# The low part of the MLP's weights: by a negation and an adding transfer, or by a subtraction

## Chip, cores and metric

The kernel runs on one core of one Trainium2 chip. The metric is the time of one execution on the device in microseconds; the lower, the better. Three executions of the kernel before were timed, and their median is the time before.

## What is computed

A trunk of two layers over 512 latent tokens and 256 context tokens, 1024 channels, float32. Each layer has one input projection, three mixers side by side (attention, mLSTM, RG-LRU), one output projection, and an MLP of 4096 channels. The last layer computes latent tokens alone.

```python
for l in range(DEPTH):
    ul, uc = modulate(rms_norm(xl), ...), modulate(rms_norm(xc), ...)
    yl, yc = token_mixing(ul, uc, ..., w_in[l], w_out[l], ...)
    xl = xl + g1l * yl
    xl = xl + g2l * squared_relu_mlp(modulate(rms_norm(xl), sh2l, sc2l), w_ff1[l], w_ff2[l])
    if l < DEPTH - 1:
        xc = xc + g1c * yc
        xc = xc + g2c * squared_relu_mlp(modulate(rms_norm(xc), sh2c, sc2c), w_ff1[l], w_ff2[l])
return rms_norm(xl, final_g)

def squared_relu_mlp(u, w1, w2):
    return jnp.square(jax.nn.relu(u @ w1)) @ w2
```

## The kernel before

Channels lie on the partitions and tokens along the columns. Every large product runs in three passes over parts of its operands: a high part, rounded to the format in which TensorE takes one pass, and a low part, the rest. `PASSES` names them: high by high, high weights by low input, low weights by high input. `dense` goes through the blocks of 128 input channels and gives all three passes of one block before the next one, so the low part of a weight tile is wanted from the third product of the tile on.

A weight tile is 128 partitions by 1024 columns of float32, 512 KB. `split_raw` (L152 to L160) brings one in: a load on SP's queue into `raw`, a cast on ScalarE into the high part `whi` (L158), and a subtraction on VectorE, `raw` less `whi`, into the low part `wlo` (L159). Each of the three names has three buffers. The buffers of `raw` are shared with other weights, among them the modulation weights `modw`, which in layer 0 are loaded beside the MLP and multiplied on VectorE.

Where these tiles are used:

- `ybc`, inside the attention stage: four tiles of `w_outc[l, 1]`, the rows of the output projection that belong to the mLSTM and the RG-LRU. Its products stand between those of the attention (scores `S`, transposes `pT`).
- `out_proj`: tiles of `w_outc[l, 0]`, the rows of the attention heads, in two sweeps over the tokens.
- `mlp`: 32 tiles of `w_ff1c` and 36 of `w_ff2c` in each layer. The first three tiles of `w_ff1c` go into `First` (L430 to L441), whose products follow the modulated input chunk by chunk as `Modulated` makes it; between them stand the sums `nps<-ones,n2acc` of the norm (L221), the reciprocal root `rsq` on POOL (L193), and its spreading over the partitions `nps<-ident,rsq` (L229). The last 8 of the 36 tiles go over the tokens in two sweeps, so that the next norm can begin on the first half while the second is still computed: 256 columns then 512 in layer 0, twice 256 in layer 1.

All products of `dense` are recorded under L186, those of `First` under L440. The order of the instructions on each engine is set by a scheduler that the program is written for; an engine takes its own instructions in that order, and waits where one is not ready. POOL has little to do: the roots of the norms, a few fills, and transfers within the mixers (L807, L917, L919).

Of the kernel before, what the change touches and what calls it, by code (L numbers as in the profile page):

```python
# [19 lines left out]
NK = 8  # L20
# [7 lines left out]
# how fast parts of the program go beside others, by layer  # L28
# [32 lines left out]
def trunk_kernel(ctx, tc, ins, out, dbg=None):  # L61
# [42 lines left out]
    # x^T, chunks of 128 channels, tokens [context | latent]  # L104
# [9 lines left out]
    # adds up rows r, 32 + r, 64 + r, 96 + r  # L114
# [6 lines left out]
    # ------------------------------------------------------------------ interleaving  # L121
    # A part of the program is a generator that yields about how long (us) what it emitted takes.
# [16 lines left out]
    def weave(*gens):  # L139
        """emit parts side by side, at equal pace; a filler only as long as the others last."""  # L140
        at = [[0.0, i, g] for i, g in enumerate(gens)]
        while any(e[2] is not filler for e in at):
            e = min(at)
            c = next(e[2], None)
            if c is None:
                at.remove(e)
            else:
                e[0] += c
                yield c

    # ---------------------------------------------------------- small helpers
    def split_raw(src, shape):  # L152
        """(hi, lo) of weights from DRAM: hi has the bits that one pass of a product carries."""
# [7 lines left out]

    def split_act(src, a, b, tag, name, shape=None, tag2=None, after=None):
        """(hi, lo) of src, into columns a:b of new tiles: hi by ScalarE, lo by VectorE."""
# [11 lines left out]
    def mm3(dst, w, r, first, last):  # L175
        """dst += w.T @ r from the (hi, lo) parts of both."""
# [3 lines left out]
    def dense(ps, wk, rk, segs, M=128, po=PO):  # L180
        """ps[:M, po + t] = sum_k wk[k].T @ rk[k][:, t]; wk, rk: lists of (hi, lo)."""
# [8 lines left out]
    def rsqrt(v, n):  # L190
        """v ** -0.5 for n columns."""
# [4 lines left out]
    class Norm:  # L196
        """(mean of squares over channels + eps) ** -0.5 of each token, on every partition."""
# [17 lines left out]
        def columns(self, seg, out=None):  # L215
            """by tokens on partitions, a column per block of 128."""
# [9 lines left out]
        def spread(self, seg, ps, y):  # L226
            """on every partition, tokens along the columns."""
# [7 lines left out]
    # ------------------------------------------------------------- modulation  # L235
# [6 lines left out]
    def mod_vec(l, v, pace):  # L242
        """one of the six modulation vectors of a layer, a step per 128 rows of its weights."""
# [24 lines left out]
    def mod_rows(rows):  # L268
        """silu of both conditions along the columns, on every partition."""
# [10 lines left out]
    def mod_dot(l, v, pace, rows):  # L280
        """one of the six modulation vectors of a layer, a step per 128 of its channels."""
# [18 lines left out]
    def mod_load(j, tags):  # L300
        """the weights of 256 channels of the first two modulation vectors of the first layer."""
# [6 lines left out]
    def mod_block(j, ws):  # L308
        """256 channels of both: four groups of rows of the weights side by side."""
# [32 lines left out]
    class Modulated:  # L342
        """(hi, lo) of rms_norm(x) * (1 + scale) + shift, for two spans of tokens that get ready one after the other."""
# [6 lines left out]
        def early(self):  # L350
            """the first span, while the products before still go over the second."""
# [7 lines left out]
        def finish(self, first):  # L359
            """the rest, each chunk followed by its products."""  # L360
# [15 lines left out]
    class Output:  # L376
        """the final norm, for two spans of tokens that get ready one after the other."""
# [34 lines left out]
    def wchunks(hl):  # L412
        return [(hl[0][:, k], hl[1][:, k]) for k in range(NK)]

    def out_proj(l, y, sweeps, norm, after):
        """the rows of w_out of the attention heads."""
# [13 lines left out]
    class First:  # L430
        """the first products of a phase, as the chunks of its input come."""
# [11 lines left out]
    # ---------------------------------------------------------- input projection  # L443
# [6 lines left out]
    def in_gates(l, u, z):  # L450
        """k_rope and the mLSTM gates, the input of the RG-LRU: steps by chunk of u first."""
# [31 lines left out]
    def in_kvq(l, u, z, t0):  # L483
        """k, v of the mLSTM with tokens on partitions; its q by channels."""
# [26 lines left out]
    def in_mla(l, u, z, t0):  # L511
        """normalized c_kv; c_q times its gain, and what its norm scales the scores with."""
# [32 lines left out]
    def in_outgates(l, u, z, t0):  # L545
        """the output gates of the two recurrent groups."""
# [15 lines left out]
    # ------------------------------------------------------------------ RG-LRU  # L562
    def lru(l, z, t0):
        wl = wp.tile([128, 2, 2, 2, 128], F32, tag="raw", bufs=3, name="lruw")
        dma(wl, ins["w_lru"][l])
        # -4 * softplus(-lam); log1p(e) = 2 atanh(e / (2 + e))
# [22 lines left out]
        for c in range(2):  # L589
# [12 lines left out]
            # r and i as 2 sigmoid - 1 = tanh(half)  # L602
# [15 lines left out]
            for d in range(2):  # L618
# [7 lines left out]
                # -expm1(2 z) = -tanh(z) (1 + exp(2 z))  # L626
# [25 lines left out]
    # ------------------------------------------------------------------- mLSTM  # L652
    R = 36

    def ml_gates(l, z):
# [13 lines left out]
        # log_sigmoid(f) = min(f, 0) - log(1 + exp(-|f|))  # L669
# [50 lines left out]
        # per-token columns: [a | WS], [WI | E]  # L720
# [11 lines left out]
        # w_old per (direction, pair of heads): the end of each chunk in the order of the scan  # L732
# [17 lines left out]
    def mlstm(l, z, t0):  # L750
# [7 lines left out]
        # k^T  # L758
# [10 lines left out]
        # states: [C | n] before each chunk, per pair of heads and direction  # L769
# [27 lines left out]
        # outputs  # L797
# [6 lines left out]
        def weights(h, d, w):  # L804
            """exp(a_s + r_t) for s up to t, transposed: keys on partitions."""
# [14 lines left out]
        def inter(h):  # L820
            """what the states before each block add, both directions."""
# [37 lines left out]
        def finish(p):  # L859
            """rms over each head of a pair, back to channels, output gate."""  # L860
# [4 lines left out]
            # 2 rsqrt(4 (mean + eps)): half of it, for sigmoid(o) = (1 + tanh(o / 2)) / 2  # L865
# [430 lines left out]
```

## Time and profile before

| what | value |
|---|---|
| time, median of 3 executions | 1648.88 us (1642.92 to 1652.01) |
| span of the profiled execution | 1647.5 us |
| TensorE busy | 1600.6 us, 97% |
| VectorE busy | 1075.7 us, 65% |
| ScalarE busy | 583.2 us, 35% |
| POOL busy | 63.6 us, 4% |

The profile gives one execution, and its span is the time of that execution from its first instruction to its last; durations below are from it. Busy shares are a mean over stages that have different limits, so the stages are read one by one. The stages that the change touches are the attention of layer 0 (280 to 404 us), the output projection and the start of the MLP (404 to 467), the MLP (467 to 967), and in layer 1 the attention (1166 to 1250), the start of the MLP (1250 to 1296), the MLP (1296 to 1612) and its last sweep (1612 to 1637).

### The profile page before, as it was taken

The page shows a single profiled execution, that of the slowest core. Times are in us where ns is not written, and L with a number is a line of the kernel's source. Part 1 is how long each engine was busy: PE and PEld are TensorE (multiplying, and loading weights), DVE is VectorE, ACT ScalarE, POOL GpSimd, SP SyncE. Part 2 cuts the span into 40 slices and gives each one's busy share as a digit, 9 for nine tenths or more (in the row PEclk, how much of TensorE's full clock was granted, in tenths as well). Part 3 has the DMA queues.
Part 4 walks back from the last instruction along what each step waited for, and adds up shares of the span by engine and source line. Part 5 has one row for each costly group of instructions (what it writes and reads, how often), then busy time and mean ns, then how long its engine had stood idle before and what let it go on. Part 6 is the DMA issues. An engine that isn't in the chain of part 4 may idle for free.

```text
span 1647.5 us, 23128 instructions
## 1 busy us (share of the span) xinstructions
PE 1600.6 (97%) x9202; PEld 1335.2 (81%) x9202; DVE 1075.7 (65%) x2122; ACT 583.2 (35%) x878; POOL 63.6 (4%) x106
## 2 busy tenths in 40 slices
PE   8998999999999999999999998999999999999997
PEld 4666897788788888888888886887788888888887
DVE  4784577766797676666666478966877644444446
ACT  4462224444442212222122146622645432323223
POOL 1201010000000000000000001101000000000000
PEclk9999999999999999999999999999999999999998
DMA  9447111101344343333333131322102323222222
GB/s 314 129 158 231 64 58 47 50 14 63 105 146 149 116 141 115 109 122 118 134 120 128 65 116 40 89 70 77 65 14 90 116 90 102 90 94 99 90 103 102
DMA packets 58587, 170.48 MB, mean 103 GB/s; under 512 B 6720, under 2 KB 19776, under 8 KB 58480
## 3 DMA queue, kind: packets, MB, share of 16 engines
q1 hardware_dynamic: 55216, 161.26, 28.6%
q0 software_dynamic: 2112, 6.70, 1.4%
q8 instruction: 72, 1.18, 0.3%
q10 hardware_dynamic: 1152, 1.05, 0.2%
q14 instruction: 35, 0.29, 0.1%
HBM read 165.44 MB, written 2.15 MB: 102 GB/s over the span
## 4 chain that ended last, share of the span: by engine, by line
PE 81%; issue 2%; DVE 2%; ACT 1%; DMA 1%; POOL 0%; POOLq 0%; DVEq 0%; ACTq 0%
PE ff L186 51%; PE inp L186 6%; PE outp L186 6%; PE first L440 3%; PE py L178 2%; PE S L998 2%; PE kvp L178 2%; PE pT L1020 1%; PE S L1002 1%; PE pn L841 1%; PE S L1000 1%; PE qrp L186 1%; DMA modjunk<-in_crow 1%; PE sT L818 1%; PE lrup L608 1%
## 5 line engine op out<-in xcount | busy, mean ns | idle before, releaser
L158 ACT CAST whi<-raw 128x1024 fp32r<-128x1024 f32 x191 | 200.6, 1051 | 721.6 <-PE ff L186 578.6
L159 DVE TENSOR_TENSOR wlo<-raw,whi 128x1024 fp32r<-128x1024 f32 x191 | 233.1, 1221 | 158.4 <-ACT whi L158 153.9
L186 PE MATMUL ff<-hh,whi 128*128 128x512 f32 (+1 forms) x800 | 242.2, 348 | 0.0
L186 PE MATMUL ff<-hl,whi 128*128 128x512 f32 (+1 forms) x800 | 242.0, 348 | 0.0
L186 PE MATMUL ff<-hh,wlo 128*128 128x512 f32 (+1 forms) x800 | 242.0, 348 | 0.0
L289 DVE SCALAR_TENSOR_TENSOR modjunk<-modw,cb 128x512 f32<-128x512 f32 x224 | 154.7, 690 | 106.3 <-DMA modw<-in_w_modT 101.3
L186 PE MATMUL ff<-uh,whi 128*128 128x512 f32 (+1 forms) x696 | 210.9, 357 | 1.0 <-ACT hrelu L1077 1.0
L186 PE MATMUL ff<-uh,wlo 128*128 128x512 f32 (+1 forms) x696 | 210.2, 356 | 0.0
L186 PE MATMUL ff<-ul,whi 128*128 128x512 f32 (+1 forms) x696 | 209.4, 355 | 0.0
L408 DVE SCALAR_TENSOR_TENSOR x<-ff,mod,x 128x256 f32<-128x256 f32 (+1 forms) x200 | 123.1, 639 | 103.1 <-PE ff L186 103.0
L186 PEld LDWEIGHTS ff<-hl,whi 128*128 128x128 f32 x800 | 150.4, 188 | 20.8
L186 PEld LDWEIGHTS ff<-hh,wlo 128*128 128x128 f32 x800 | 150.3, 188 | 20.6
L186 PEld LDWEIGHTS ff<-hh,whi 128*128 128x128 f32 x800 | 150.3, 188 | 20.5
L186 PEld LDWEIGHTS ff<-uh,whi 128*128 128x128 f32 x696 | 130.8, 188 | 21.8 <-ACT hrelu L1077 1.7
L186 PEld LDWEIGHTS ff<-uh,wlo 128*128 128x128 f32 x696 | 131.0, 188 | 20.6 <-DVE wlo L159 0.5
L186 PEld LDWEIGHTS ff<-ul,whi 128*128 128x128 f32 x696 | 130.7, 188 | 20.5
L186 PE MATMUL inp<-uh,whi 128*128 128x256 f32 (+1 forms) x224 | 71.6, 376 | 3.7 <-ACT whi L158 3.7
L186 PE MATMUL inp<-ul,whi 128*128 128x256 f32 (+1 forms) x224 | 69.1, 366 | 0.0
L186 PE MATMUL inp<-uh,wlo 128*128 128x256 f32 (+1 forms) x224 | 68.8, 364 | 0.3 <-DVE wlo L159 0.3
L193 POOL TENSOR_TENSOR rsq<-rsv,nhalf 128x2 f32<-128x2 f32 (+2 forms) x16 | 14.2, 886 | 1310.1 <-DVE rsv L223 1308.6
L178 PE MATMUL kvp<-whi,uh 128*128 128x256 f32 x192 | 60.0, 313 | 4.2 <-ACT sig L613 2.9
L440 PE MATMUL first<-uh,wlo 128*128 128x256 f32 (+3 forms) x192 | 61.9, 325 | 0.6 <-DVE wlo L159 0.6
(316 smaller groups left out, 2767.2 us busy)
## 6 DMA issues: line engine op xcount, KB each, us to landing
raw<-in_w_ff2c SPq DMA_DIRECT2D x72, 512.0 KB, 3.5
raw<-in_w_ff1c SPq DMA_DIRECT2D x64, 512.0 KB, 3.5
modw<-in_w_modT SPq DMA_DIRECT2D x56, 512.0 KB, 3.7
modw<-in_w_mod SPq DMA_DIRECT2D x24, 512.0 KB, 4.4
raw<-in_w_outc SPq DMA_DIRECT2D x24, 512.0 KB, 3.5
raw<-in_w_inc SPq DMA_DIRECT2D x21, 512.0 KB, 3.5
modw<-in_w_mod SPq DMA_DIRECT2D x32, 256.0 KB, 5.1
raw<-in_w_inkv SPq DMA_DIRECT2D x8, 512.0 KB, 3.5
```

The source lines that it names most:

```text
L158: nc.scalar.copy(hi, raw)
L159: V.tensor_tensor(lo, raw, hi.bitcast(F32), op=OP.subtract)
L178: mm(dst, w[a], r[b], start=first and i == 0, stop=last and i == 2)
L186: mm(ps[:M, po + t0:po + t1], wk[k][a], rk[k][b][:, t0:t1], start=(k == 0 and i == 0), stop=(k == n - 1 and i == 2))
L289: V.scalar_tensor_tensor(junk, w[:, 512 * i:512 * i + 512], 1.0, rows[2 * r + i], op0=OP.mult, op1=OP.mult, accum_out=acc[:, m, i, r:r + 1])
L408: V.scalar_tensor_tensor(x[m][:, s[0]:s[1]], ps[:, po + s[0]:po + s[1]], modv[l][:, v, m, r:r + 1], x[m][:, s[0]:s[1]], op0=OP.mult, op1=O ...
L440: mm(ps[:M, PO + s[0]:PO + s[1]], wk[k][a][:, :M], self.rk[k][b][:, s[0]:s[1]], start=(k == 0 and i == 0), stop=(k == NK - 1 and i == 2))
L608: mm(ps[:, PO + a:PO + b], wl[:, g, d, c], xs[:, a:b], start=True, stop=True)
L818: mm(sT[h][:, PO + 128 * b:PO + 128 * b + 128], kT[p][hp, bs], z["q"][p][hp, bs], start=True, stop=True)
L841: mm(w["pn"][:, 65 * b:65 * b + 65], wT[:, 128 * b:128 * b + 128], z["vt"][p][:, b, j], start=True, stop=True)
L998: mm(S[:, PO + a:PO + e], z["qk"][h][wa][:, qs], ckv[ra][:, a:e], start=(i == 0), stop=False)
L1000: mm(S[:, PO + a:PO + e], z["qr"][h][:, qs], kr[0][:, a:e], start=False, stop=False)
```

## The change

A second helper stands beside `split_raw`. It loads `raw` in the same way. ScalarE writes the negated value into `wlo`, in the format of the high part; a transfer from SBUF to SBUF on POOL's queue then adds `raw` to what stands in `wlo`; and ScalarE casts the high part as before. VectorE takes no part. `ybc` and `mlp` use it, 72 tiles in each layer; `out_proj`, the input projection and the others stay with `split_raw`. Line numbers below the new helper grow by 10 or 11.

```diff
+    def split_dma(src, shape):
+
+        raw = wp.tile(shape, F32, tag="raw", bufs=3, name="raw")
+        dma(raw, src)
+        hi = wp.tile(shape, F32R, tag="whi", name="whi")
+        lo = wp.tile(shape, F32R, tag="wlo", name="wlo")
+        nc.scalar.activation(lo, raw, AF.Copy, scale=-1.0)
+        gdma(lo, raw, accum_op=OP.add)
+        nc.scalar.copy(hi, raw)
+        return hi, lo
...
-                first = First([wchunks(split_raw(ins["w_ff1c"][l, i], [128, NK, 128])) for i in range(3)], u, [128] * 3)
+                first = First([wchunks(split_dma(ins["w_ff1c"][l, i], [128, NK, 128])) for i in range(3)], u, [128] * 3)
...
-                w = wchunks(split_raw(ins["w_ff1c"][l, f * FB + i], [128, NK, 128]))
+                w = wchunks(split_dma(ins["w_ff1c"][l, f * FB + i], [128, NK, 128]))
...
-                    w = split_raw(ins["w_ff2c"][l, f, mp], [128, 2, FB, 128])
+                    w = split_dma(ins["w_ff2c"][l, f, mp], [128, 2, FB, 128])
...
-                    w = split_raw(ins["w_outc"][l, 1, mp], [128, 2, 4, 128])
+                    w = split_dma(ins["w_outc"][l, 1, mp], [128, 2, 4, 128])
```

The scheduler gives the engines a new order. ScalarE where the attention of layer 0 begins to use the tiles of `w_outc[0, 1]`, before (`yBCh` is the high part of the inputs of these products, `pr` the softmax, `pTh` its transpose):

```order
L167 CAST wuvh<-raw 128x512
L158 CAST whi<-raw 128x1024
L167 CAST yBCh<-o 128x768
L158 CAST whi<-raw 128x1024
L167 CAST yBCh<-o 128x768
L1008 ACT_TABLE_LOAD
```

and after:

```order
L178 CAST wuvh<-raw 128x512
L168 ACTIVATE wlo<-raw 128x1024
L178 CAST yBCh<-o 128x768
L170 CAST whi<-raw 128x1024
L178 CAST yBCh<-o 128x768
L1019 ACT_TABLE_LOAD
```

The negation of the first tile stands where its cast stood, its cast stands where the second tile's cast stood, and the second tile comes later in the stage.

TensorE at the start of the MLP of layer 0, around the sums of the latent tokens' norm, before (`first_4063`, `first_4064` and `first_4065` are the sums of the first three tiles, in that order):

```order
L440 MATMUL first_4065<-uh_3910,whi_4059 128x256
L440 MATMUL first_4065<-ul_3911,whi_4059 128x256
L440 MATMUL first_4065<-uh_3910,wlo_4060 128x256
L221 MATMUL nps_4118<-ones_86,n2acc_3707 128x1 x4
L440 MATMUL first_4063<-uh_3912,whi_4047 128x256
L440 MATMUL first_4064<-uh_3912,whi_4053 128x256
L440 MATMUL first_4065<-uh_3912,whi_4059 128x256
```

and after (the first three tiles are now `first_4070`, `first_4071` and `first_4072`):

```order
L451 MATMUL first_4071<-uh_3914,wlo_4059 128x256
L451 MATMUL first_4070<-uh_3916,whi_4051 128x256
L451 MATMUL first_4071<-uh_3916,whi_4058 128x256
L232 MATMUL nps_4125<-ones_86,n2acc_3711 128x1 x4
L451 MATMUL first_4070<-ul_3917,whi_4051 128x256
L451 MATMUL first_4070<-uh_3916,wlo_4052 128x256
L451 MATMUL first_4071<-ul_3917,whi_4058 128x256
```

The products of the third tile's low part, of which four stood ahead of the sums, now all stand behind them, the first of them 13 rows on; ahead of the sums stand 28 products of `First` instead of 36.

POOL from the end of the mixers of layer 0 to the end of its MLP, before (`rsq<-rsv` are the roots of the norms):

```order
L193 TENSOR_TENSOR rsq<-hms,nhalf 128x12
L193 TENSOR_TENSOR rsq<-rsv,nhalf 128x2
L193 TENSOR_TENSOR rsq<-rsv,nhalf 128x4
L193 TENSOR_TENSOR rsq<-rsv,nhalf 128x2
L456 MEMSET xp 128x2
```

and after:

```order
L204 TENSOR_TENSOR rsq<-hms,nhalf 128x12
L169 DMA wlo<-raw 128x1024 x4
L204 TENSOR_TENSOR rsq<-rsv,nhalf 128x2
L169 DMA wlo<-raw 128x1024 x3
L204 TENSOR_TENSOR rsq<-rsv,nhalf 128x4
L169 DMA wlo<-raw 128x1024 x65
L204 TENSOR_TENSOR rsq<-rsv,nhalf 128x2
L467 MEMSET xp 128x2
```

The 72 adding transfers of the layer now stand between the roots, and each of them waits for its negation.

## Rows read from the trace of the kernel before

**Rows 1.** The page, busy time, share of the span and instructions of each engine.
```profile
PE 1600.6 (97%) x9202; PEld 1335.2 (81%) x9202; DVE 1075.7 (65%) x2122; ACT 583.2 (35%) x878; POOL 63.6 (4%) x106
```

**Rows 2.** The page, the chain that ended last, its shares of the span by engine.
```profile
PE 81%; issue 2%; DVE 2%; ACT 1%; DMA 1%; POOL 0%; POOLq 0%; DVEq 0%; ACTq 0%
```

**Rows 3.** By stage: length, busy PE, PEld, DVE, ACT, POOL (x count), PEclk, DMA, GB/s.
```profile
280.00:404.00 124.00, 120.75 (x740) 100.23 (x739) 88.25 (x187) 61.22 (x123) 0.00 (x0) 0.99 0.09 33
404.00:467.00 63.00, 59.67 (x328) 51.02 (x327) 50.86 (x95) 28.79 (x46) 1.80 (x2) 0.97 0.33 113
467.00:910.00 443.00, 443.00 (x2537) 387.86 (x2536) 306.46 (x653) 103.44 (x115) 0.00 (x0) 1.00 0.37 129
...
1166.00:1250.00 84.00, 83.42 (x488) 67.30 (x488) 61.46 (x122) 42.08 (x84) 0.00 (x0) 1.00 0.13 43
1250.00:1296.00 46.00, 43.82 (x357) 42.16 (x355) 37.59 (x76) 24.25 (x46) 1.50 (x2) 1.00 0.30 104
1296.00:1612.00 316.00, 316.00 (x1367) 256.54 (x1368) 145.22 (x177) 95.19 (x121) 0.00 (x0) 1.00 0.28 99
1612.00:1637.00 25.00, 24.13 (x201) 23.73 (x199) 21.75 (x44) 11.60 (x22) 0.70 (x1) 1.00 0.26 91
```

**Rows 4.** The page, groups: line engine operation x count | busy, mean ns | idle before.
```profile
L158 ACT CAST whi<-raw 128x1024 fp32r<-128x1024 f32 x191 | 200.6, 1051 | 721.6 <-PE ff L186 578.6
L159 DVE TENSOR_TENSOR wlo<-raw,whi 128x1024 fp32r<-128x1024 f32 x191 | 233.1, 1221 | 158.4 <-ACT whi L158 153.9
```

**Rows 5.** Timeline of ScalarE: start, us, operation [idle before <-releaser].
```profile
936.03 1.06 ACT L158 CAST whi<-raw 128x1024 fp32r<-128x1024 f32 x1 [7.29 <-PE ff L186]
...
1600.87 1.06 ACT L158 CAST whi<-raw 128x1024 fp32r<-128x1024 f32 x1 [4.49 <-PE ff L186]
...
1620.68 1.05 ACT L158 CAST whi<-raw 128x1024 fp32r<-128x1024 f32 x1 [1.18 <-issue]
...
1623.49 1.05 ACT L158 CAST whi<-raw 128x1024 fp32r<-128x1024 f32 x1 [1.14 <-PE ff L186]
```

**Rows 6.** Queue of SP's loads; transfers, median landing in us; line L917 (`sig<-kg`, POOL).
```profile
q1 hardware_dynamic: 55216, 161.26, 28.6%
...
raw<-in_w_ff2c SPq DMA_DIRECT2D x72, 512.0 KB, 3.5
...
sig<-kg POOLq DMA_DIRECT2D x2, 192.0 KB, 4.3
...
DMA to landing us min/median/max: 4.2/7.2/10.2
```

**Rows 7.** Timeline at the start of the attention's output products, layers 0 and 1.
```profile
282.88 1.04 ACT L158 CAST whi<-raw 128x1024 fp32r<-128x1024 f32 x1
...
286.92 0.38 PE L186 MATMUL outp<-yBCh,wlo 128*128 128x256 f32 x1 [0.58 <-DVE wlo L159]
...
1163.99 2.00 ACT L158 CAST whi<-raw 128x1024 fp32r<-128x1024 f32 x2
...
1167.25 0.51 PE L186 MATMUL outp<-yBCh,wlo 128*128 128x512 f32 x1 [0.21 <-DVE wlo L159]
```

**Rows 8.** Timeline at the start of the MLP, layers 0 and 1.
```profile
433.35 1.05 ACT L158 CAST whi<-raw 128x1024 fp32r<-128x1024 f32 x1 [0.48 <-PE outp L186]
438.90 1.05 ACT L158 CAST whi<-raw 128x1024 fp32r<-128x1024 f32 x1 [0.87 <-PE outp L186]
438.94 0.28 PE L440 MATMUL first<-uh,whi 128*128 128x256 f32 x1
443.18 0.95 PE L221 MATMUL nps<-ones,n2acc 128*128 128x1 f32 x8
...
1271.32 1.05 ACT L158 CAST whi<-raw 128x1024 fp32r<-128x1024 f32 x1 [0.51 <-PE outp L186]
1276.63 0.39 PE L440 MATMUL first<-uh,wlo 128*128 128x256 f32 x1 [0.57 <-DVE wlo L159]
1279.38 0.50 PE L221 MATMUL nps<-ones,n2acc 128*128 128x1 f32 x4
```

## The prediction

> **What bounds the kernel now.** I read the engines' busy shares first: TensorE works 97% of the span of 1647.5 us, VectorE 65%, ScalarE 35% [rows 1]. The chain that ended last says the same from behind: 81% of it is TensorE, and VectorE holds 2% [rows 2]. So work that leaves VectorE gives back time only where TensorE stands and waits for it, and the table by stage shows where that can be [rows 3]. In the two long stretches of the MLP, 467 to 910 us and 1296 to 1612 us, TensorE is busy to the last microsecond; a VectorE that is freed there gives nothing. What is left for a gain is TensorE's idle time in the other stages with changed tiles: 3.25 us (280 to 404), 3.33 (404 to 467), 0.58 (1166 to 1250), 2.18 (1250 to 1296) and 0.87 (1612 to 1637), together 10.2 us. Of this the trace puts 0.58, 0.21 and 0.57 us on a `wlo` subtraction at the three places that I looked at [rows 7, 8]. The question of the change is therefore the other one: does the low part now come later than TensorE asks for it, and where does nothing hide that?
>
> **What is removed and added.** 144 of the 191 tiles change (4 of w_outc, 32 of w_ff1c, 36 of w_ff2c in each layer). VectorE loses 144 subtractions of 1.221 us, 176 us of its 1075.7 [rows 1, 4]. ScalarE gains 144 negations. No row shows a negation of this shape; the cast of the same tile takes 1.051 us [rows 4], and I take that: 151 us, ScalarE then at 734 us or 45%. Both are off the path except at the places below. POOL issues 144 transfers. The order on POOL puts three of them ahead of the reciprocal root of the latent tokens' norm in layer 0; the last of the three waits for a negation that ends at about 441.0 us, and the statistics that the root needs are begun on TensorE at 443.18 [rows 8]. That cover of some 2 us makes it free; were it gone, the norm would follow one to one.
>
> **The price that decides, L**: the time from the end of the negation until the low part has landed. Before, the high part ends, and 1.22 us later the low part is there; now a negation of 1.05 us and L stand between. No row shows an adding transfer. From below, a plain load of the same 512 KB lands after 3.5 us [rows 6]. From above, the slowest transfer between SBUF tiles on POOL's queue took 10.2 us (192 KB, in a burst of six) [rows 6]. The nearest row is the same transfer in layer 1, 4.3 us for 192 KB [rows 6]. The other 320 KB I add at the rate of the loads: 161.26 MB in 28.6% of 1647.5 us is 342 GB/s [rows 1, 6], so 0.96 us, and L is 5.3 us, an estimate. I take 5.3 because that row has both things that the new transfer has, the queue and SBUF at both ends.
>
> The Trainium skill speaks against the change here: "Collectives: The Full Stack", section "Part 3: Why 7× under link rate — side-by-side accounting", says that an adding transfer has to read two sources and was measured at about half the rate of a copy. No row here shows one; by that rule the moving part of 512 KB at 342 GB/s, 1.5 us, would count twice, an estimated L of 6.8, and the sum would come to about 1668 us.
>
> **Where L is hidden.** In the main stretches a tile lasts 1.06 + 7.29 = 8.35 us in layer 0 and 1.06 + 4.49 = 5.55 us in layer 1 on TensorE, read from ScalarE's casts, each of which waits for TensorE to give a buffer back [rows 5]. With three buffers a negation can start when tile n is done, and its result is wanted two tiles on, 16.7 or 11.1 us later. 1.05 + 5.3 = 6.35 us fits in both: nothing, as long as L stays under about 10 us in layer 1. In layer 0 the `raw` buffers are shared with 56 loads of modulation weights, so the margin is smaller than 16.7, but 467 to 910 us has time.
>
> **Where it is not hidden**, at L = 5.3:
> - Attention, layer 0. The first cast of w_outc starts at 282.88; the negation takes its place on ScalarE, ends at 283.92, the low part lands at 289.2. The product that needs it stands fifth in its group before and after, and ran at 286.92 [rows 7]: +2.3 us.
> - Attention, layer 1. The first of two casts starts at 1163.99, now a negation that ends at 1165.0; landed at 1170.3 against 1167.25 [rows 7]: +3.1 us. TensorE idles 0.58 us in all of this stage [rows 3], so nothing takes that up.
> - Start of the MLP, layer 0. The second tile's cast starts at 433.35 and the negation follows it: 435.45, landed at 440.75. TensorE begins the first products at 438.94 and does one in (443.18 - 438.94)/36 = 0.118 us [rows 8], so the sixth, which needs that tile, is due at 439.53: +1.2 us. The third tile's cast at 438.90 becomes cast and negation, done at 441.0, landed at 446.3. The new order puts 12 products between the norm's sums, which now stand after 28 products instead of 36, and its first product: due at 438.94 + 1.2 + 40 x 0.118 + 0.9 (the sums) = 445.8, +0.5 us. Together 1.7.
> - Start of the MLP, layer 1. Second tile: 1271.32 + 2 x 1.05 + 5.3 = 1278.7. From there 12 products lead to the norm's sums, 1.4 us, so these start at 1280.1 against 1279.38 [rows 8]: +0.7 us. The wait of 0.57 us for the subtraction at 1276.63 is already replaced in this.
> - The last sweeps of the second weights, 256 columns wide: a tile every 1623.49 - 1620.68 = 2.81 us [rows 5]. A `raw` buffer is now held for 3.5 + 1.05 + 5.3 = 9.85 us; three buffers give a tile each 3.28 us, 0.47 too slow. Eight tiles go at this pace at the end and four in layer 0; three of each run are ahead when it starts, so 6 x 0.47 = +2.8 us.
>
> VectorE's relief in the sweeps I put at -0.5 us, about half of the 0.87 us that TensorE idles there [rows 3]. The sum: 2.3 + 3.1 + 1.7 + 0.7 + 2.8 - 0.5 = +10.1 us on the span of 1647.5, so 1657.6. The median of the runs shown, 1648.88, is 1.4 us over that span; carried over, 1659 us. About 0.5% (8 us) is what a measurement of this kernel can tell from no change, so this is only just slower.
>
> **Rivals.**
> A, not slower: the adding transfer lands like the plain load, L = 3.5. Then the attention costs 0.5 + 1.3, the starts of the MLP nothing, the sweeps nothing (8.05/3 = 2.68 per tile): +1.3 us, 1650. At L = 4.3 it is 1.3 + 2.1 + 0.2 + 0.8 - 0.5 = +3.9, 1653. It stays within 0.5% up to about L = 4.7. For it: both ends are in SBUF. Against: the 192 KB row is already at 4.3.
> B, the addition is slow. At L = 7 the same terms are 4.0 + 4.8 + 3.4 + 2.4 + 6.2 - 0.5 = +20, 1669; at 10.2 they are 7.2 + 8.0 + 6.6 + 5.6 + 12.7 = +40, 1689. For it: the row of 10.2 us [rows 6], and the transfer has to read what it adds to.
> C, paced by the transfer: above L = 10 a low-part buffer in layer 1 is held for longer than three tiles; at L = 12 (1.05 + 12 + 5.55 - 3 x 5.55)/3 = 0.65 us on some 60 tiles, 39 us, and 45 at the places above: about 1733. No row is that slow.
> D, the relief wins: VectorE, free at the starts of the MLP, brings norms and modulated inputs forward, and L is at most 4. The waits shown for subtractions are 1.4 us, the idle time that could go is 10.2: 1639 to 1648. Against it: most of that idle time has other releasers.
> That the change doesn't do what it says would show as VectorE still at 1075 us; the order shows the subtractions gone, so I give it no chance of its own.
>
> **How the numbers follow.** Chances: forecast (L from 4.7 to 7, 1655 to 1669) 0.45, of which 0.12 ends below 1657.1; A 0.27; B above L = 7 0.17; C 0.05; D 0.06, half of it under 1640.6. So faster by over 0.5% 0.03, within 0.5% 0.12 + 0.27 + 0.03 = 0.42, slower 0.33 + 0.17 + 0.05 = 0.55. The likeliest case gives 1659. The range holds the forecast, A, half of D and nearly all of B: 1646 to 1690. It leaves out C and the ends of B and D, about 0.1 to 0.15.
>
> **What would show it.** The median time to landing of the adding transfer is L; everything scales with it. At 289 and 1170 us TensorE should wait for a transfer for 2 to 4 us, at the second tile of each MLP start for about a microsecond, in the last sweep tiles should be 3.2 to 3.3 us apart; the two main stretches should still show TensorE fully busy. I am wrong if the main stretch of layer 1 shows gaps (L over 10), if the norm's root on POOL waits behind a transfer, or if the issue itself holds POOL for much longer than a fraction of a microsecond, so that transfers queue up.

## The result and the profile after

The changed kernel takes 1706.57 us in the median of five executions (1694.4 to 1712.34), against 1648.88 us: a ratio of 1.035, with an interval of 1.031 to 1.039. Run once more (e11 below) the ratio was 1.0395 (1.0364 to 1.0425). The direction was forecast, the size was not: 1659 us stood there, and the range ended at 1690.

The page of the changed kernel, profiled in the execution that took 1694.4 us, the fastest of the five, so that the account by stage explains 45.1 us where the medians lie 57.7 apart: busy times; DMA queues with packets, MB and share of 16 engines; chain by engine; the transfer's group on POOL; and transfers with their size and median time to landing in us.

```profile
PE 1610.5 (95%) x9202; PEld 1344.6 (79%) x9202; DVE 913.7 (54%) x1978; ACT 713.0 (42%) x1022; POOL 191.2 (11%) x250
...
q1 hardware_dynamic: 55216, 161.26, 28.9%
q0 software_dynamic: 22848, 82.21, 26.1%
...
PE 66%; issue 11%; DMA 7%; DVE 2%; ACT 1%; POOL 1%; POOLq 0%; SPq 0%; DVEq 0%; ACTq 0%
...
L169 POOL DMA_DIRECT2D wlo<-raw x144 | 127.0, 882 | 915.4 <-ACT wlo L168 887.7
...
wlo<-raw POOLq DMA_DIRECT2D x144, 512.0 KB, 5.4
raw<-in_w_ff2c SPq DMA_DIRECT2D x72, 512.0 KB, 4.3
raw<-in_w_ff1c SPq DMA_DIRECT2D x64, 512.0 KB, 4.4
```

VectorE lost 162 us and ScalarE gained 130 [rows 1], a little less than the 176 and 151 that counts by means of groups gave. TensorE is busy for 95% of a longer span. The adding transfer lands after 5.4 us in the median. The chain now runs through TensorE for 66% instead of 81% [rows 2], and DMA and issue hold 18%.

The table by stage, cut where the same work begins and ends as in [rows 3] (length, busy PE, PEld, DVE, ACT, POOL with counts, PEclk, DMA share, GB/s):

```profile
281.00:412.00 131.00, 124.49 (x774) 105.31 (x775) 86.95 (x190) 66.11 (x130) 3.56 (x4) 0.96 0.22 57
412.00:470.00 58.00, 52.92 (x278) 43.99 (x276) 41.02 (x82) 27.53 (x43) 4.67 (x5) 1.00 0.46 127
470.00:540.00 70.00, 61.82 (x340) 53.41 (x340) 38.16 (x95) 28.09 (x33) 8.15 (x9) 0.95 0.77 203
540.00:920.00 380.00, 380.00 (x2177) 332.57 (x2175) 205.10 (x503) 124.03 (x137) 40.66 (x46) 1.00 0.69 186
920.00:985.00 65.00, 60.88 (x364) 53.10 (x363) 21.47 (x41) 26.12 (x33) 9.99 (x12) 1.00 0.68 156
...
1186.00:1275.00 89.00, 85.24 (x491) 69.04 (x492) 57.69 (x119) 46.16 (x90) 3.41 (x4) 0.98 0.25 66
1275.00:1322.00 47.00, 43.90 (x353) 43.08 (x351) 33.15 (x72) 24.85 (x46) 4.14 (x5) 0.96 0.48 135
1322.00:1640.00 318.00, 311.45 (x1334) 251.96 (x1335) 76.86 (x117) 147.39 (x180) 50.55 (x58) 0.98 0.82 187
1640.00:1677.00 37.00, 30.75 (x194) 28.43 (x193) 12.02 (x27) 18.20 (x26) 6.78 (x9) 0.91 0.88 197
```

The span grew by 45.1 us. TensorE's idle time accounts for 35.2 of it (46.9 us before, 82.1 after), and its busy time for 9.9 (1600.6 and 1610.5), with as many products at a granted clock of 0.979 instead of 0.988. By stage, in us, forecast and found:

| stage | idle before | idle after | more | forecast |
|---|---|---|---|---|
| attention, layer 0 | 3.25 | 6.51 | 3.3 | 2.3 |
| output projection and start of the MLP, layer 0 | 3.33 | 5.08 | 1.8 | 1.7 |
| main stretch, layer 0 | 0.00 | 8.18 | 8.2 | 0 |
| sweeps, layer 0 | 0.08 | 4.12 | 4.0 | 0.5 |
| attention, layer 1 | 0.58 | 3.76 | 3.2 | 3.1 |
| start of the MLP, layer 1 | 2.18 | 3.10 | 0.9 | 0.7 |
| main stretch, layer 1 | 0.00 | 6.55 | 6.5 | 0 |
| sweeps, layer 1 | 0.87 | 6.25 | 5.4 | 1.8 |
| the rest | 36.6 | 38.5 | 1.9 | 0 |
| TensorE's busy time | | | 9.9 | 0 |

(The forecast for the sweeps was 2.8 - 0.5 us, six steps of 0.47; one of the six lay in layer 0.) At the places at which a low part was expected late the idle time is right to within a microsecond or so, but in layer 0 partly by luck (below). The loss that was missed lies in the two stretches that I took as covered, in the sweeps, and in the clock.

**The start of the main stretches.** TensorE in the timeline of the changed kernel, at the first uses of each kind (start, us, operation, [idle before <-releaser]):

```profile
283.11 0.76 PE L197 MATMUL outp<-yBCh,whi 128*128 128x256 f32 x2 [2.72 <-ACT whi L170]
...
288.86 0.58 PE L197 MATMUL outp<-yBCh,wlo 128*128 128x256 f32 x1 [4.36 <-DMA wlo<-raw]
...
441.72 0.39 PE L451 MATMUL first<-uh,wlo 128*128 128x256 f32 x1 [2.90 <-DMA wlo<-raw]
...
1191.41 0.79 PE L197 MATMUL outp<-yBCh,wlo 128*128 128x512 f32 x1 [3.65 <-DMA wlo<-raw]
...
1303.82 0.43 PE L451 MATMUL first<-uh,wlo 128*128 128x256 f32 x1 [2.21 <-DMA wlo<-raw]
...
475.49 1.01 PE L197 MATMUL ff<-uh,whi 128*128 128x256 f32 x2 [5.43 <-ACT whi L170]
477.80 1.01 PE L197 MATMUL ff<-uh,wlo 128*128 128x256 f32 x2 [1.30 <-DMA wlo<-raw]
...
1328.03 0.80 PE L197 MATMUL ff<-uh,whi 128*128 128x512 f32 x1 [4.62 <-ACT whi L170]
...
1330.51 0.79 PE L197 MATMUL ff<-uh,wlo 128*128 128x512 f32 x1 [1.26 <-DMA wlo<-raw]
```

The second to fifth rows are the forecast places: the products of the attention ran at 286.92 and 1167.25 before [rows 7], and waited 0.58 and 0.21 us. In layer 0 the waits were longer than forecast, 4.36 us in the attention and 2.90 at the start of the MLP, because the low parts came late there, 7.4 and 7.2 us after the ends of their negations at 281.39 and 434.49 us, where L was put at 5.3:

```profile
280.34 1.05 ACT L168 ACTIVATE wlo<-raw 128x1024 fp32r<-128x1024 f32 x1
...
433.44 1.05 ACT L168 ACTIVATE wlo<-raw 128x1024 fp32r<-128x1024 f32 x1
```

The first row of TensorE's timeline is a wait of 2.7 us that was not forecast, for a high part that was cast behind the negation at 280.34. The idle time grew by only 3.3 and 1.8 us because other waits became shorter or went: the norm's spreading waited 1.7 us for the root on POOL instead of 3.1, and a wait of 1.8 us for the attention's inputs is gone.

The last four rows are new. Where the products of `First` end, its three weight tiles let go of their buffers within 1.4 us, and only then can the next tiles be negated. ScalarE at that place in layer 0:

```profile
467.26 1.05 ACT L170 CAST whi<-raw 128x1024 fp32r<-128x1024 f32 x1 [7.36 <-PE first L451]
468.21 1.50 ACT L1088 ACTIVATE hrelu<-first 128x768 f32<-128x768 f32 x2
469.61 1.57 ACT L1089 ACTIVATE hrelu<-hrelu 128x768 f32<-128x768 f32 x2
471.07 0.81 ACT L1088 ACTIVATE hrelu<-first 128x768 f32<-128x768 f32 x1
471.76 1.06 ACT L168 ACTIVATE wlo<-raw 128x1024 fp32r<-128x1024 f32 x1
472.71 0.84 ACT L1089 ACTIVATE hrelu<-hrelu 128x768 f32<-128x768 f32 x1
473.44 1.06 ACT L168 ACTIVATE wlo<-raw 128x1024 fp32r<-128x1024 f32 x1
474.39 1.04 ACT L170 CAST whi<-raw 128x1024 fp32r<-128x1024 f32 x1
```

The high part of the fourth tile is cast at once (467.26; the tiles are counted from the first of `First`). Its negation comes after five passes of the squared ReLU over the three results of `First`, at 471.76; the fifth tile's high part, which TensorE wants next, is cast behind a further negation and done at 475.4; the fourth tile's low part lands just before 477.80. Before, three casts and three subtractions on two engines did this, and TensorE did not stop: 443.00 us busy of 443.00 [rows 3].

**The clock.** The same table in narrow stretches around that place:

```profile
460.00:469.00 9.00, 8.84 (x39) 6.83 (x37) 5.89 (x16) 1.74 (x3) 0.00 (x0) 1.00 0.37 117
469.00:476.00 7.00, 1.50 (x6) 1.11 (x6) 6.22 (x14) 6.43 (x9) 1.79 (x2) 0.90 0.24 47
476.00:478.00 2.00, 0.70 (x3) 0.21 (x2) 0.42 (x1) 0.00 (x0) 0.00 (x0) 0.50 1.00 166
478.00:480.00 2.00, 2.00 (x7) 1.71 (x8) 0.00 (x0) 0.00 (x0) 0.00 (x0) 0.50 0.99 225
480.00:482.00 2.00, 2.00 (x10) 1.72 (x9) 0.00 (x0) 0.00 (x0) 0.00 (x0) 0.65 1.01 258
482.00:484.00 2.00, 2.00 (x13) 1.78 (x12) 0.05 (x1) 1.18 (x2) 0.00 (x0) 1.00 0.90 277
```

TensorE was busy for 1.50 us of the 7 before 476, and the granted clock then is half, 1.2 of 2.4 GHz, to 480, and in part to 482, although from 477.80 on TensorE does not stop. These 4.2 us hold the work of about 2.4. A pair of products of 256 and 512 columns, which the timeline gives as one row, takes 1.01 us at 477.80, where such a row took 0.51 us before:

```profile
467.35 0.51 PE L186 MATMUL ff<-uh,wlo 128*128 128x256 f32 x2
```

The sum had no such term.

**The sweeps.** POOL in the last sweep, the issues of the adding transfers:

```profile
1650.33 0.86 POOL L169 DMA_DIRECT2D wlo<-raw  x1 [4.73 <-ACT wlo L168]
1654.85 0.86 POOL L169 DMA_DIRECT2D wlo<-raw  x1 [3.66 <-ACT wlo L168]
1659.36 0.86 POOL L169 DMA_DIRECT2D wlo<-raw  x1 [3.64 <-ACT wlo L168]
1664.00 0.86 POOL L169 DMA_DIRECT2D wlo<-raw  x1 [3.78 <-ACT wlo L168]
1668.76 0.86 POOL L169 DMA_DIRECT2D wlo<-raw  x1 [3.90 <-DMA raw<-in_w_ff2c]
```

The tiles are 4.5 to 4.8 us apart; the pace of the products is 2.81 [rows 5], and my buffer cycle gave 3.28. The DMA engines are full here, and the loads on SP wait for the adding transfers to give their `raw` buffers back (first row: 1655 to 1674 us; second row: SP's waits, 1645 to 1672 us):

```profile
1655.00:1674.00 19.00, 13.50 (x91) 12.98 (x91) 6.33 (x16) 10.68 (x16) 4.50 (x6) 0.87 0.99 228
```

```profile
SPq L165 <- DMA wlo<-raw: 23.6, 5, 6.3
```

Two sums come near 4.5. The first is of the engines. POOL's queue took 26.1% of 1692.6 us, 441.8 us of all 16 engines; less the 23.1 us of its old transfers (1.4% of 1647.5) this is 2.91 us for each of the 144. A load takes 28.9% of 1692.6 us for 161.26 MB, so 1.59 us for 512 KB. Together 4.50 us per tile: more than the sweep's 2.81, and 81% of the 5.55 us of a tile in layer 1, where the table shows 0.82. The second is the forecast's own: a buffer is held from the issue of its load to the landing of its transfer, and for the last five tiles that was 12.1 to 15.8 us (1652.02 to 1664.25 us, for one) instead of 9.85, in the mean 13.7, a third of which is 4.6. The two are not independent, since loads and transfers take longer on full engines; no run holds one of them fixed.

### The profile page after: what moved, and what is told of

It is laid out like the page before. It is cut to its first block, busy times and chain, and to the rows that moved or that the text cites. A ratio compares the mean times of both kernels' runs of the same rounds, so it can differ in the third digit from the quotient of the medians.

```text
span 1692.6 us, 23466 instructions
## 1 busy us (share of the span) xinstructions
PE 1610.5 (95%) x9202; PEld 1344.6 (79%) x9202; DVE 913.7 (54%) x1978; ACT 713.0 (42%) x1022; POOL 191.2 (11%) x250
## 3 DMA queue, kind: packets, MB, share of 16 engines
q1 hardware_dynamic: 55216, 161.26, 28.9%
q0 software_dynamic: 22848, 82.21, 26.1%
## 4 chain that ended last, share of the span: by engine, by line
PE 66%; issue 11%; DMA 7%; DVE 2%; ACT 1%; POOL 1%; POOLq 0%; SPq 0%; DVEq 0%; ACTq 0%
PE ff L197 42%; PE inp L197 6%; PE first L451 4%; DMA wlo<-raw 3%; PE outp L197 3%; PE kvp L189 2%; DMA modw<-in_w_modT 2%; PE S L1009 1%; PE py L189 1%; PE pn L852 1%; PE pT L1031 1%; DVE modjunk L300 1%; PE S L1013 1%; DMA raw<-in_w_ff2c 1%; PE sT L829 1%
## 5 line engine op out<-in xcount | busy, mean ns | idle before, releaser
L169 POOL DMA_DIRECT2D wlo<-raw x144 | 127.0, 882 | 915.4 <-ACT wlo L168 887.7
L197 PE MATMUL ff<-uh,whi 128*128 128x512 f32 (+1 forms) x696 | 213.1, 361 | 11.1 <-ACT whi L170 10.1
L168 ACT ACTIVATE wlo<-raw 128x1024 fp32r<-128x1024 f32 x144 | 151.5, 1052 | 14.2 <-DMA raw<-in_w_ff1c 9.4
L1092 DVE CAST hh<-hrelu 128x768 fp32r<-128x768 f32 (+1 forms) x64 | 34.0, 531 | 143.7 <-ACT hrelu L1089 143.5
L159 DVE TENSOR_TENSOR wlo<-raw,whi 128x1024 fp32r<-128x1024 f32 x47 | 57.3, 1219 | 33.3 <-ACT whi L158 32.7
```

The lines of the kernel that those rows point to most:

```text
L159: V.tensor_tensor(lo, raw, hi.bitcast(F32), op=OP.subtract)
L168: nc.scalar.activation(lo, raw, AF.Copy, scale=-1.0)
L169: gdma(lo, raw, accum_op=OP.add)
L197: mm(ps[:M, po + t0:po + t1], wk[k][a], rk[k][b][:, t0:t1], start=(k == 0 and i == 0), stop=(k == n - 1 and i == 2))
L1092: V.tensor_copy(hi[:, t0:], t[:, t0:])
```

## The experiments

Each kernel was timed beside the kernel before on the same chip; ratios are to that. The theories: A, the low part lands late at the places that nothing covers, and each pays its wait; B, the transfers load the DMA engines or hold buffers, so that everything else comes late too; C, ScalarE's own work and order are the cause.

| run | what | median us | ratio to before, interval |
|---|---|---|---|
| e1 | no adding transfer | 1648.40 | 1.0021 (1.0001 to 1.0040) |
| e2 | overwriting instead of adding | 1677.57 | 1.0194 (1.0171 to 1.0217) |
| e3 | three tiles after First undone | 1691.37 | 1.0263 (1.0202 to 1.0323) |
| e4 | changed in the main stretches only | 1655.88 | 1.0062 (1.0034 to 1.0089) |
| e5 | changed in layer 1's main stretch only | 1645.35 | 1.0002 (0.9980 to 1.0024) |
| e6 | sweeps undone | 1688.41 | 1.0247 (1.0197 to 1.0298) |
| e7 | attention undone | 1698.89 | 1.0311 (1.0277 to 1.0346) |
| e8 | e4 without modulation loads | 1649.17 | 1.0014 (1.0001 to 1.0028) |
| e9 | First undone | 1697.04 | 1.0310 (1.0272 to 1.0349) |
| e10 | each transfer in two halves | 1705.35 | 1.0332 (1.0289 to 1.0374) |
| e11 | the changed kernel again | 1713.56 | 1.0395 (1.0364 to 1.0425) |
| e12 | e4, adding from DRAM | 1650.18 | 1.0035 (1.0017 to 1.0053) |

### e1: the transfer left out

```diff
         nc.scalar.activation(lo, raw, AF.Copy, scale=-1.0)
-        gdma(lo, raw, accum_op=OP.add)
         nc.scalar.copy(hi, raw)
```

> The changed kernel without the adding transfer: the low part holds the negated high part, the weights are never added to it. ScalarE's negations, its new order and VectorE's relief stay, POOL's 144 transfers and their 75 MB go. Theory A (the low part lands late at places where nothing covers it) and theory B (the transfer loads the DMA engines, so that all weights land late) both expect the time of before, 1640 to 1655 us. Theory C (ScalarE's extra 151 us and its new order hold TensorE up) expects over 1670 us.

The ratio is 1.0021: theory C falls, and with it any hope in VectorE's relief. With the subtractions gone and nothing in their place but the negation, the kernel is no faster than before. What is left of the new waits is the part that ScalarE's order makes: 2.7 us in the attention of layer 0, for the cast behind the negation, and these at the two starts of the main stretches:

```profile
464.83 0.62 PE L196 MATMUL ff<-uh,wlo 128*128 128x256 f32 x2 [2.83 <-ACT wlo L168]
...
1291.31 0.50 PE L196 MATMUL ff<-uh,wlo 128*128 128x512 f32 x1 [2.22 <-ACT wlo L168]
```

Here TensorE waits for the negation itself, 2.83 and 2.22 us, and not for a transfer; so of the 6.7 and 5.9 us that it waits at these places in the changed kernel, ScalarE's order alone makes less than half (TensorE's own order differs there too: here it takes the fourth tile's low part before the fifth tile's high part). Over the whole span TensorE idles for 48.6 us (1643.4 - 1594.8) against 46.9 before, so about 6 us of other waits went.

### e2: overwriting instead of adding

```diff
-        gdma(lo, raw, accum_op=OP.add)
+        gdma(lo, raw)
```

> The transfer overwrites the low part with the weights instead of adding to it; all dependences, issues and bytes written stay, only the read of what stands there goes. The low part is then wrong by the high part. Theory B expects the 16 DMA engines to be busy with POOL's queue for about half as long (13% of the span instead of 26%), loads of the weights back at about 3.7 us to landing, and a time of 1670 to 1690 us. Theory A with a landing time that is mostly fixed expects a landing of 5 us and 1695 us or more.

Of its page, POOL's queue; of the line of the transfer, its issue on POOL (shortest, median and longest, in ns) and its time to landing, first in this run and then in the changed kernel:

```profile
q0 software_dynamic: 22848, 82.21, 14.2%
```

```profile
L169 POOL DMA_DIRECT2D wlo<-raw x144: 527/527/794, 282.7 to 1655.0; - x144
...
DMA to landing us min/median/max: 2.9/3.1/6.9
```

```profile
L169 POOL DMA_DIRECT2D wlo<-raw x144: 852/869/1139, 281.7 to 1671.3; - x144
...
DMA to landing us min/median/max: 4.5/5.4/8.2
```

The queue's share falls from 26.1 to 14.2%: (237.7 - 23.1)/144 = 1.49 us of the 16 engines per transfer instead of 2.91. Adding costs them 1.95 times what a copy of the same bytes does. The issue falls from 0.869 us to 0.527, the landing from 5.4 us to 3.1, the loads' landing from 4.3 and 4.4 us back to 3.5. So about half of the loss is what the addition costs over a copy. The Trainium skill, "Collectives: The Full Stack", section "Part 3: Why 7× under link rate — side-by-side accounting", says of the adding step of a reduce-scatter that it reads two sources and runs at about half the rate of a copy. The trace agrees with the rate, at 1.95, for a transfer within one core; that the second reading is the reason is not shown by a run here. In the last sweep the tiles of this run are 2.9 to 4.4 us apart, 3.6 in the mean, where the engines' sum is 1.62 + 1.49 = 3.1: here the engines' sum alone does not give the pace.

### e3, e6, e7, e9: each uncovered place undone by itself

```diff
e3  -w = wchunks(split_dma(ins["w_ff1c"][l, f * FB + i], ...))
e3  +w = wchunks((split_raw if f * FB + i < 6 else split_dma)(ins["w_ff1c"][l, f * FB + i], ...))
e6  -w = split_dma(ins["w_ff2c"][l, f, mp], ...)
e6  +w = (split_raw if f == NF // FB - 1 else split_dma)(ins["w_ff2c"][l, f, mp], ...)
e7  -w = split_dma(ins["w_outc"][l, 1, mp], ...)
e7  +w = split_raw(ins["w_outc"][l, 1, mp], ...)
e9  -first = First([wchunks(split_dma(ins["w_ff1c"][l, i], ...)) ...
e9  +first = First([wchunks(split_raw(ins["w_ff1c"][l, i], ...)) ...
```

> The three tiles of the first weights that follow the products of First in each layer come by the subtraction again, all others stay changed. In the profile of the changed kernel TensorE waits 5.43 + 1.30 us and 4.62 + 1.26 us there, 12.6 us together. Theory A expects 12 to 16 us less than the changed kernel, so a ratio to before of about 1.026 to 1.028. Theory B expects that the waits come back with the next tiles, less than 5 us gained, a ratio over 1.031.

> The changed kernel with the eight tiles of each layer's last sweeps back on the subtraction. In the profile TensorE idles 4.1 us (layer 0, 920 to 985) and 6.2 us (layer 1, 1640 to 1677) there, against 0.1 and 0.9 before. Theory A expects 9 us less than the changed kernel from the idle time and 2 to 4 us from the clock that comes back: a ratio to before of about 1.027. If the delay only moves on to what follows, over 1.033.

> The changed kernel with the four tiles of w_outc in each layer's attention back on the subtraction. The profile shows waits of 4.4 and 3.6 us for the transfer there and 2.7 us for a cast behind a negation. Theory A expects 6 to 10 us less than the changed kernel, a ratio of 1.029 to 1.031; that other engines' work fills the time would give 1.034.

> The changed kernel with the three tiles of First in each layer back on the subtraction. Its profile shows waits of 2.9 us (layer 0) and 2.8 us (layer 1) for the transfer there. Theory A expects 5 to 7 us less than the changed kernel, a ratio to before of 1.030 to 1.032.

Against 1.035 to 1.0395 for the changed kernel, e3 gives back 0.9 to 1.3% (14 to 22 us), e6 1.0 to 1.5% (17 to 24), e7 0.4 to 0.8% (6 to 14) and e9 0.4 to 0.9% (7 to 14). Each lies near or above what was expected. Undone together, in e4, they give back 2.9 to 3.3%, all but 0.6% of the loss. So the loss lies at the uncovered places; that it is their plain sum fits (2.7 to 4.5%), but intervals of some half a per cent to each side do not show it. Why they give back more than their idle time is shown for e3 alone: its profile idles for 68.6 us instead of 82.1, and TensorE's busy time is 1603.8 us at 0.986, where the changed kernel has 1610.5 at 0.979. In the profiles of e6, e7 and e9 the busy time is 1610.9, 1615.0 and 1613.3 us, no lower than in the first profile, so there the rest stays open. Theory B, taken as a delay of everything everywhere, falls with e4: 108 of the 144 transfers are still there, and 0.6% is lost.

### e4, e5, e8, e12: the main stretches alone

e4 is e3, e6, e7 and e9 at once. e5 keeps the change in layer 1 only; e8 takes the modulation weights' loads out of e4; e12 lets the addition in e4 read DRAM:

```diff
e5  +... (split_raw if f * FB + i < 6 or not l else split_dma)(...) ...
e5  +... (split_raw if f == NF // FB - 1 or not l else split_dma)(...)
e8  -w = wp.tile([128, D], F32, tag="raw", bufs=3, name="modw")
e8  -dma(w, ins["w_modT"][6 * l + v - NMR, m])
e8  -V.scalar_tensor_tensor(junk, w[:, 512 * i:512 * i + 512], 1.0, rows[2 * r + i], ...
e8  +V.scalar_tensor_tensor(junk, rows[0], 1e-4, rows[2 * r + i], ...
e12 -gdma(lo, raw, accum_op=OP.add)
e12 +gdma(lo, src, accum_op=OP.add)
```

> Only the 54 tiles of each layer's MLP that lie in the main stretches come by negation and adding transfer; the four tiles in the attention, the six at the start of the MLP and the eight of the last sweeps come by the subtraction. Theory A expects every wait gone, 1646 to 1656 us. Theory B expects that the traffic of 108 transfers still delays loads, 1665 us or more.

> As e4_main_loops_only, but in layer 1 alone: 54 tiles by negation and adding transfer, every other tile by the subtraction. In e4 all of TensorE's wait in the MLP lies in layer 0, for VectorE, which waits for modulation weights. Theory B1 (a raw buffer is kept longer, and the modulation weights that share these buffers come late) expects 1644 to 1650 us, a ratio to before of 0.998 to 1.003. Theory B2 (the traffic itself slows TensorE or the loads everywhere) expects a ratio of 1.004 or more.

> As e4_main_loops_only, with the 56 loads of modulation weights beside the MLP of layer 0 left out; VectorE's 224 products of them run on a tile that stays, so the modulation of layer 1 has wrong values. Theory B1 expects TensorE's wait for VectorE in layer 0, 11.9 us in e4, to be gone and a time of 1640 to 1648 us. If the adding transfers delay the MLP's own weights, the wait stays: 1655 us.

> As e4_main_loops_only, but the adding transfer reads the weights from DRAM instead of from raw, so that a raw buffer is free once ScalarE has read it twice, while the DMA engines have as much to do or more. In e4 VectorE waits 187 us for modulation weights beside the MLP of layer 0, against 101 us before. Theory B1 (the raw buffers are kept too long) expects that wait back near 100 to 120 us, TensorE's wait for VectorE gone, and a ratio to before of 0.999 to 1.003. Theory B3 (the DMA engines are loaded by the adding transfers, and the modulation weights' loads wait for them) expects the wait to stay over 160 us and the ratio at 1.005 or more.

In e5 the change is free: 54 transfers in layer 1, DMA engines at 0.81, TensorE busy for 316.00 us of 316.00, ratio 1.0002. That bears out what the prediction said of a covered stretch. In e4, with layer 0 as well, 0.6% is lost. That is at the end of theory A's range, but not every wait is gone: this one is left in the MLP of layer 0 (first row, e4), and e12 shortens it (second row):

```profile
PE ff L197 <- DVE x L419: 11.9, 6, 8.8
```

```profile
PE ff L197 <- DVE x L419: 7.0, 4, 2.7
```

It is a chain through VectorE: the products of the modulation weights (`modjunk`) stand on VectorE ahead of the additions that empty TensorE's accumulators, and they wait for their loads. e8, without these loads, has no such wait and a ratio of 1.0014 (1649.17 us, a microsecond above the range expected), so the loads are the cause. What delays them is settled less well. With raw buffers that need not wait for the transfer (e12) TensorE's wait falls from 11.9 to 7.0 us and its longest from 8.8 to 2.7, and the ratio to 1.0035, between the two expectations; VectorE's own wait for these loads stays, 183 us against 187. That number tells less than I expected of it: VectorE has less else to do in this stretch, 239.8 us of work from 467 to 910 us in e12 against 306.46 before [rows 3], and so more time to wait. The transfer from DRAM also lands later, after 7.5 us instead of 5.6. Both the buffers and the engines' load seem to count; their shares stay open.

### e10 and e11: halves, and the kernel again

```diff
-        gdma(lo, raw, accum_op=OP.add)
+        n = shape[1] // 2
+        gdma(lo[:, :n], raw[:, :n], accum_op=OP.add)
+        gdma(lo[:, n:], raw[:, n:], accum_op=OP.add)
```

> Each adding transfer is split into two of 512 columns, 288 in all; the bytes are the same. Theory A1 (the landing time as such) expects the first half to land about 1.2 us earlier and TensorE to wait about that much less at each of the some twelve waits: a ratio to before of about 1.025. Theory A2 (the whole tile's landing counts, or POOL's issue of 0.87 us per transfer grows to 1.2 us and more for the pair) expects no gain, 1.034 or more.

> The changed kernel once more, as it is. Its runs lay between 1694 and 1712 us, and its profile is of the fastest; TensorE waits 1.4 us there for VectorE behind modulation weights, while the profiles of e4_main_loops_only and e7_attention_undone show 11.9 us of that wait. Theory B1 expects that a profile of a slower run shows this wait, 8 to 14 us, and that it makes up the distance of the median to the fastest run. Otherwise all waits of the first profile are some 30% longer.

The first halves do land earlier, after 3.6 us in the median. The time is 1705.35 us where e11 on the same chip has 1713.56; the intervals touch (up to 1.0374, from 1.0364), so a gain of some 10 us (0.6%) is possible and not shown. The ratio of 1.0332 lies near A2's 1.034 and far from A1's 1.025, so A1 falls as it was priced. The second halves land after 6.2 us, later than a whole tile, and the pair of issues holds POOL for longer than the 1.2 us expected: 0.869 us in the median for the first half, as long as for a whole tile, and 1.23 for the second.

e11's profile is of an execution of 1706.22 us, 11.8 us longer than that of the first profile. TensorE's busy time is 1616.6 us (6.1 more, at 0.975), and of 5.7 us more idle time 4.6 are the wait for VectorE, 6.0 us instead of 1.4. So the wait behind the modulation weights does vary from execution to execution, but it is less than the 8 to 14 us expected, and half of the spread is the clock. Why it varies was not looked into further.

## Why the prediction was wrong

- **What bounds the kernel: right.** VectorE's time gives nothing back on balance. e1, where the subtractions are gone and no transfer takes their place, stands at 1.0021.
- **L: near in the median, short where it counted.** 5.3 us was estimated, and from issue to landing 5.4 us is the median, from 4.5 to 8.2. L was meant from the end of the negation, and so it is 5.8 us in the median, from 4.8 to 8.5: 7.4 in the attention of layer 0 (281.39 to 288.82), 7.2 at the start of its MLP (434.49 to 441.68), and 5.8 in the attention of layer 1 (1185.57 to 1191.36). The 6.8 us that the prediction worked out from the two readings is nearer at the first two.
- **The places named as uncovered: right in place, short in size.** 10.1 us were forecast for attention, starts and sweeps; 18.6 were found as idle time. In layer 0 the attention and the start of the MLP came out near the forecast by luck: longer waits for the low part and a late cast, against waits that became shorter elsewhere.
- **"Where L is hidden": this step failed.** It took the steady state of three buffers for the whole main stretch. At its start all three buffers come free nearly at once, and the first tiles have neither the lead nor ScalarE to themselves. 8.2 us (1.4 of them a wait for VectorE) and 6.5 us stood there instead of nothing, and e3 gives back 14 to 22 us. The gaps in the main stretches that the prediction named as a sign of L over 10 did come, with an L of at most 8.5.
- **The sweeps: the term was mis-sized.** A tile was priced by how long a buffer is held, 9.85 us or 3.28 per tile, with loads and transfers as fast as on quiet engines. But load and transfer need 1.59 + 2.91 = 4.50 us of the 16 DMA engines per tile, so on full engines both take longer, a buffer is held for 12.1 to 15.8 us, and the tiles came 4.5 to 4.8 us apart. The prediction gave the rule of the two readings one sentence, as 1.5 us more of latency; measured, it is also 1.4 us more of the engines for every tile.
- **The clock: missing.** 9.9 us in the first profile, 16.0 in e11's (1616.6 - 1600.6). It goes with the waits: e4 and e8, with few of them, have 1599.4 and 1597.3 us of busy time.
- **"467 to 910 us has time" for the modulation weights: wrong by 0.6%** (e4 against e5 and e8).
- **POOL's queue ahead of the norm's root: right, at nothing.** The root of layer 0 starts at 446.12 us and waits for VectorE, not behind a transfer.
- **Rival B** named a slow addition as the way to 1669 to 1689 us. At two of the named places the low part did come as late as B's 7 us. But most of the loss that was missed lies where B had no term, at the starts of the main stretches and in the clock, and the range did not allow for what the engines' time does to a sweep.
- **Rival C's sum** is short by its own terms: at L = 12 the places named come to about 50 us and not 45, so about 1738 us. Nothing hangs on it.

## What to carry to other kernels

A cover computed from the steady state of a ring of buffers does not hold where the ring starts or where all of its buffers come free together; look at that place by itself. A transfer that is moved into a stage is priced twice, once by its landing where someone waits, and once by the DMA engines' time per tile against the pace of the stage; where that time is over the pace, landings and the time that buffers are held grow too. An engine at 65% that no wait leads to is not worth relieving: leave the new cost out altogether (as in e1) and see whether anything is gained before paying for it.

## What the runs showed of the hardware

An adding transfer of 512 KB from SBUF to SBUF took 2.91 us of the 16 DMA engines, against 1.49 us for the overwriting one, and its issue held POOL for 0.869 us against 0.527; the first of two issues of half the size (e10) held it for 0.869 us too. After a stretch in which it was busy for 1.50 us of 7, TensorE had a granted clock of 0.50 for some 4 us, and 1.00 again after 2 us more at 0.65, so that such a pair of waits, 6.7 us together, cost about 2 us more than its length.
